# A mixture of experts whose first eight pairs' rows are scattered to two planes in memory and read back

## The chip, the core and the metric

The kernel runs on one core of one Trainium2 chip. The metric is the time on the device in microseconds (us), the median of several runs. A trace of one more execution is read with it.

## What is computed

A decoder block for 512 tokens of width 1024, float32. Two token mixers share one input projection, a sparse attention and a sliding-window attention; their gated sum goes through an output projection, a residual and a layer norm. Then comes the part that the change touches, a mixture of 32 experts in 4 groups. Each token takes its best group and in it its two best experts:

```python
g_sel = jnp.argmax(g_logits, axis=-1)
top_p, top_i = lax.top_k(e_prob, EXPERT_TOPK)            # 2 of the 8 experts of the group
top_w = g_w * top_p / top_p.sum(-1, keepdims=True)
expert_id = g_sel[:, None] * EXPERTS_PER_GROUP + top_i
...
for e in range(N_EXPERTS):
    h = jax.nn.silu(xt @ w_gate[e]) * (xt @ w_up[e])
    out = out + combine[:, e:e + 1] * (h @ w_down[e])
...
x = layer_norm(ALPHA * x + ffn, ln2_g[layer], ln2_b[layer])
```

## The kernel before

Attention and router take the first 415 us or so. They matter here only where the start of the program is spoken of: the input arrives as `xraw` and `wraw`, the index keys of the sparse attention are written to `pgA` and copied to the other 64 partitions by a transfer (`pgA<-pgA`), and the index scores (`qk<-pgA,qs`) read them.

**Experts.** Experts w and w+16 are a pair, and a pair is a job: each expert has 64 slots, so a job has 128 rows. The jobs run in the order 0 to 7, an overflow tile `ov` for tokens over 64, 8 to 15. The list `work` holds that order, n is the place in it: pair 9 is n = 10. For a job

- `gather` (GpSimd) reads the 128 slots' rows of `x1d` from memory by an index per slot; a slot without a token has an index past the end;
- `transposed` turns them on TensorE in eight transposes (`qt<-ident,xg`), and ScalarE copies them out as `xg`;
- `up_proj` makes 32 products (`mm<-wexp,xg`) with the two experts' gate and up weights, ScalarE takes SiLU, VectorE multiplies (`h`);
- `turn_hidden` turns `h` in two transposes (`mm<-ident,h`), ScalarE copies out `hT`;
- `down_half`, twice, makes 16 products (`pv<-wexp,hT`);
- the rows go back to their tokens by products too: `down_proj` splits the weighted rows into two parts `yh` and `yl`, `places` makes a matrix `ct` of zeros and ones (which slot holds which token), and `combine` multiplies, `qt<-yh,ct` and `qt<-yl,ct`, for four blocks of 128 tokens and two halves: 16 products and eight adds into the residual `acc` on VectorE. These eight parts, the list `late`, run inside the next job: HEAD = 4 after its up products, four after its hidden transposes.

**Weights.** Each expert's weights are three pages of 1 MiB, two up and one down, so a job has four up and two down loads. They are issued by SyncE in the order of use, three jobs ahead (`stage`), into a ring of 22 pages that also holds all else; a load waits until a page's last reader has passed. Banks tagged `qt` (four) hold the transposed rows and the combining products in turn.

**Order.** Inside an engine a scheduler fixes the order of instructions when the program is built; in time an engine runs them strictly in that order. DMAs of one queue start in the order of issue.

Of the kernel before, what the change touches and what calls it, by code (L numbers as in the profile page):

```python
# [10 lines left out]
F32 = mybir.dt.float32  # L11
# [9 lines left out]
P = 128  # L21
D = 1024
T = 512
# [45 lines left out]
KEEP1 = 15  # L69
KEEP1_E = ('tensor', 'scalar', 'vector')  # L70
HEAD = 4
LAST_N = (0, 1, 1, 2, 1, 2, 1, 0)
P_TR = 0
P_UP = 0
# [51 lines left out]
def block_kernel(ctx: ExitStack, tc: tile.TileContext, xT, x, w_tm, w_in, w_uv, w_br, w_out, relb, oh,  # L126
# [17 lines left out]
    def mm_bank():  # L144
        return bank("mm", 2)
# [104 lines left out]
    nc.vector.memset(ones, 1.0)  # L250
    rank4 = const.tile([P, 4], F32, name="rank4")
    nc.vector.tensor_scalar(rank4, iot[:, 0:4], -1.0, 5.0, op0=ALU.mult, op1=ALU.add)
    info = const.tile([P, NB, 16, 5], BF16, name="info")
    nc.vector.tensor_copy(info[:, :, :, 0:1], part1[:, None, None, :].to_broadcast([P, NB, 16, 1]))
    for b in range(NB):
        nc.vector.memset(info[:, b, :, 1:2], float(b))
    ident = const.tile([P, P], F32, name="ident")
# [16 lines left out]
    drb = dram.tile([8, 384], F32, name="drb")  # L274
    ska = dram.tile([8, P, 256], F32, name="ska")
    skb = dram.tile([8, P, 512], F32, name="skb")


    w_load_upto(1)
# [409 lines left out]
    for h in range(8):  # L689
        if h + 1 < 8:  # L690
            need(f"q{h + 1}")
            lg[h + 1] = dsa_logits(h + 1)
        if h and h % 2 == 0:
            dsa_up(h // 2 - 1)
        if h in BR_AT:
            br_load(BR_AT.index(h))
        for j in PREP_AT.get(h, ()):
            br_prep(j)
        dsa_out(h, lg.pop(h))
    fill(2)  # L700
    dsa_up(3)
# [39 lines left out]


    sel = const.tile([P, NB, NE], BF16, name="sel")
    wts = const.tile([P, NB, NE], F32, name="wts")
    key = const.tile([P, NB, NE], F32, name="key")
    lgt = const.tile([P, NB, 36], F32, name="lgt")
    lgm = const.tile([P, NB, NE], F32, name="lgm")
    tops = const.tile([P, 2, NB], F32, name="tops")
    wrt = const.tile([P, KC, 36], F32, name="wrt")
    nc.sync.dma_start(wrt, w_rt.rearrange("p (k c) -> p k c", k=KC))  # L750
# [148 lines left out]
    def route_weights():  # L899
# [18 lines left out]
        for c in range(3):  # L918
            nc.vector.tensor_copy(info[:, :, :, 2 + c], wp)
            if c < 2:  # L920
                nc.vector.tensor_sub(wp, wp, info[:, :, :, 2 + c])

    tok = const.tile([P, 16], F32, name="tok")
    wsl = const.tile([P, 16], F32, name="wsl")
    idx = const.tile([P, 16], I32, name="idx")

    def slots(i0, i1, weighted=True):

        pi = qk_bank()
        v = small.tile([P, 2, 8], F32, name="sl", bufs=2)  # L930
        c = slice(i0, i1)
        Gs = []

        def collect(a, n):
            for i, G in enumerate(Gs):
                for b in range(NB):
                    nc.tensor.matmul(pi[:, i * 8 + a:i * 8 + n], G[:, b], info[:, b, i0 + i, a:n], start=(b == 0),
                                     stop=(b == NB - 1))
            nc.vector.tensor_copy(v[:, :, a:n], pi[:, 0:16].rearrange("p (i c) -> p i c", c=8)[:, :, a:n])

        def weights():
            nc.vector.tensor_add(wsl[:, c], v[:, :, 2], v[:, :, 3])
            nc.vector.tensor_add(wsl[:, c], wsl[:, c], v[:, :, 4])

        for i in range(i0, i1):
            G = temp(BF16, "G")[:, 0:T].rearrange("p (b s) -> p b s", b=NB)
            kv = key.rearrange("p b (s e) -> p b s e", s=2)[:, :, :, i:i + 1]
            nc.vector.tensor_tensor(G.rearrange("p b (s c) -> p b s c", s=2),
                                    iot[:, None, None, 0:CAP].to_broadcast([P, NB, 2, CAP]),
                                    kv.to_broadcast([P, NB, 2, CAP]), ALU.is_equal)  # L950
            Gs.append(G)
        collect(0, 5 if weighted else 2)
        nc.vector.scalar_tensor_tensor(tok[:, c], v[:, :, 1], 128.0, v[:, :, 0], op0=ALU.mult, op1=ALU.add)
        nc.vector.tensor_scalar(v[:, :, 5], tok[:, c], 0.0, 4096.0, op0=ALU.is_equal, op1=ALU.mult)
        nc.vector.scalar_tensor_tensor(idx[:, c], tok[:, c], -1.0, v[:, :, 5], op0=ALU.add, op1=ALU.add)
        if weighted:
            weights()
        else:
            return lambda: (collect(2, 5), weights())

    x1d = dram.tile([T, D], F32, name="x1d")
    first = [pv_bank(), pv_bank()]
# [19 lines left out]
    def run(parts, n):  # L982
        for _ in range(n):
            if parts:
                parts.pop(0)()
# [70 lines left out]

    def gather(ix, m=P):

        pg = xgs[len(gathers) % 3]
        nc.gpsimd.memset(pg, 0.0)  # L1060
        gathers.append(nc.gpsimd.indirect_dma_start(out=pg[0:m], out_offset=None, in_=x1d[:, :],
                                                    in_offset=bass.IndirectOffsetOnAxis(ap=ix, axis=0),
                                                    bounds_check=T - 1, oob_is_err=False))
        return pg
# [16 lines left out]
            banks.append(tp)  # L1081
        return evac_x(banks, xgs[3])

    def up_proj(xt, up, ph=None, parts=(), counts=LAST_N, w_=None):

        ph = ph or mm_bank()
        for k in range(KC):
            for s in range(2):
                c = (k % 4) * T
                if len(up) == 2:  # L1090
                    Pinned(P_UP).matmul(ph[s * 64:(s + 1) * 64], xt[k][:, s * 64:(s + 1) * 64], up[s][k // 4][:, c:c + T],
                                     start=(k == 0), stop=(k == KC - 1))
                else:
                    Pinned(P_UP).matmul(ph[s * 64:(s + 1) * 64, 0:256], xt[k][:, 0:64],
                                     up[0][k // 4][:, c + s * 256:c + (s + 1) * 256],
                                     start=(k == 0), stop=(k == KC - 1))
            run(parts, counts[k])
        h = temp(F32, "h")
        if len(up) == 2:
            nc.scalar.activation(h[:, 0:256], ph[:, 0:256], AF.Silu)  # L1100
            if w_ is None:
                nc.vector.tensor_mul(h[:, 0:256], h[:, 0:256], ph[:, 256:512])  # L1102
            else:
                nc.vector.scalar_tensor_tensor(h[:, 0:256], h[:, 0:256], w_, ph[:, 256:512], op0=ALU.mult, op1=ALU.mult)
            return h[:, 0:256]
        h = h[64:128, 0:256]
        nc.scalar.activation(h, ph[0:64, 0:256], AF.Silu)
        nc.vector.tensor_mul(h, h, ph[64:128, 0:256])
        return h

    def turn_hidden(h, n):
        m = n * CAP
# [19 lines left out]
    def down_proj(hT, dn, w_):  # L1132
# [21 lines left out]
            r.append((yy,))  # L1154
        return r

    def places(tk_):
        ct = temp(F32R, "ct", "pt")
        nc.vector.tensor_scalar(ct, iot, tk_, None, op0=ALU.is_equal)
        return ct  # L1160
# [30 lines left out]

    def overflow_tiles():

        pn = mm_bank()
        for b in range(NB):
            nc.tensor.matmul(pn[:, 0:NE], ones, sel[:, b], start=(b == 0), stop=(b == NB - 1))
        nc.vector.tensor_copy(cnt, pn[:, 0:NE])
# [21 lines left out]
    def overflow_tile(j):  # L1219
# [21 lines left out]
        for c, m_ in enumerate((og, ow)):  # L1241
            nc.vector.tensor_add(m_[:, :, 0], m_[:, :, 0], m_[:, :, 1])
            nc.vector.tensor_copy(m_[:, :, 1], m_[:, :, 0])
            po = mm_bank()
            for b in range(NB):
                nc.tensor.matmul(po[:, 0:2], m_[:, b].rearrange("p z c -> p (z c)"), tv[:, b], start=(b == 0), stop=(b == NB - 1))
            nc.vector.tensor_copy(so[:, c:c + 1], po[:, c:c + 1])
        nc.vector.tensor_scalar(so[0:CAP, 2:3], so[0:CAP, 0:1], 0.0, 4096.0, op0=ALU.is_equal, op1=ALU.mult)
        io = small.tile([P, 1], I32, name="ovi_", bufs=1)
        nc.vector.scalar_tensor_tensor(io[0:CAP], so[0:CAP, 0:1], -1.0, so[0:CAP, 2:3], op0=ALU.add, op1=ALU.add)  # L1250
        pg = gather(io[0:CAP, 0:1], CAP)
        up = [page(F32, "wup") for _ in range(2)]
        dn = page(F32, "wdn")
        for q in range(2):
# [13 lines left out]
    def stage(w):  # L1268
        if w == "ov":
            jobs[w] = overflow_tile(0.0)  # L1270
        else:
            pg = None
            if w:
                pg = gather(idx[:, w:w + 1])
            if w == 15:
                load_pieces(6 * w + G2_AT)
                nc.sync.dma_start(g2[:, 0:D], bcast(ln2_g, D))
# [2 lines left out]
            es = (w, w + 16)  # L1280
            jobs[w] = (pg, [ups[e] for e in es], [dns[e] for e in es], tok[:, w:w + 1], wsl[:, w:w + 1])

    for w in work[:2]:
        stage(w)
    route_weights()
    weights()
    slots(2, 4)
    stage(work[2])
    late = []
    sums = small.tile([P, NB, 2], F32, name="sums", bufs=1)  # L1290
    mv4 = small.tile([P, 4, NB + 1], F32, name="mv4", bufs=1)
# [52 lines left out]
    def rest(pz, fresh=False):  # L1344
# [25 lines left out]
        for hf in range(2):  # L1370
# [4 lines left out]
        nc.gpsimd.indirect_dma_start(out=out[:, :], out_offset=bass.IndirectOffsetOnAxis(ap=idx[:, 15:16], axis=0),  # L1375
                                     in_=zs[:, 0:D], in_offset=None, bounds_check=T - 1, oob_is_err=False)

    for n, w in enumerate(work):
        if n % 2 == 0 and 4 + n < 16:
            slots(4 + n, 6 + n)  # L1380
# [3 lines left out]
            g2 = page(F32, "ln2")  # L1384
        if n + 3 < len(work):
            stage(work[n + 3])
        pg, up, dn, tk_, w_ = jobs.pop(w)
        last = n + 1 == len(work)
        if last:

# [5 lines left out]
            zb = [page(F32, "zb") for _ in range(2)]  # L1396
            z4 = [zb[b // 2][:, (b % 2) * D:(b % 2 + 1) * D] for b in range(NB)]
            pz = [tr_bank() for _ in range(2)]
        h = up_proj(xt.pop(w), up, None if n else pv_bank(), late if last else (), LAST_N, w_ if last else None)
        run(late, KC if last else HEAD)  # L1400
        if last:
            if DEV_E == 1:
                deviations(slice(0, 2))
            pick(pz, [0])
        if n < TR_FIRST:
            xt[work[n + 1]] = transposed(jobs[work[n + 1]][0], 1)
        hT = turn_hidden(h, len(up))
        run(late, KC)
        if last and DEV_E == 2:
            deviations(slice(0, 2))  # L1410
        if not last:
            if work[n + 1] not in xt:
                xt[work[n + 1]] = transposed(jobs[work[n + 1]][0], n >= PIN_N or n in PIN_S)
            y = down_proj(hT, dn, w_)
            late = combine(places(tk_), y, then if n + 2 == len(work) else None)
    pick(pz, [1], [0])
    for hf in range(2):
        down_half(hT, dn, hf, pz[hf])
# [6 lines left out]
    nov = nc.values_load(novi[0:1, 0:1], min_val=0, max_val=15)  # L1425
    with tc.For_i(1, nov, 1):
        o = overflow_tile(jc)
        y = down_proj(turn_hidden(up_proj(transposed(o[0]), o[1]), 1), o[2], o[4])
        parts_of.clear()
        run(combine(places(o[3]), y, then), 8)  # L1430
        pz = [tr_bank() for _ in range(2)]
# [93 lines left out]
```

## Time and profile before

| | us |
|---|---|
| median of 3 runs (710.46 to 710.7) | 710.65 |
| the profiled execution | 711.01 |
| its span in the trace | 709.2 |
| TensorE busy | 679.0 (96%) |
| VectorE busy | 430.3 (61%) |
| ScalarE busy | 268.2 (38%) |
| GpSimd busy | 83.9 (12%) |

The busy shares are means over the whole span. In the experts, from about 420 us to 690 us, the 16 DMA engines are busy too, which this table does not show.

### The profile page before, as it was taken

To read this page: it belongs to the slowest core of one execution; us is meant where nothing else is said; L and a number is where in the kernel's file an instruction comes from. 1 tells how busy PE (TensorE), PEld (TensorE's weight loads), DVE (VectorE), ACT (ScalarE), POOL (GpSimd) and SP (SyncE) were. 2 spreads that over 40 slices of the span, in tenths; PEclk is the share of its full clock that TensorE was granted. 3 is DMA by queue.
4 is the path that set the end of the run, shared out by engine and by line. 5 is a ranking of instruction groups with operands and counts; after the bars stand their busy time and mean duration, and the time that the engine had idled before them with its cause. 6 is when DMAs were issued, how large, how long until landed. Compare 5 with 4: busy or idle time off the path is not lost.

```text
span 709.2 us, 9623 instructions
## 1 busy us (share of the span) xinstructions
PE 679.0 (96%) x3522; PEld 459.3 (65%) x3522; DVE 430.3 (61%) x1018; ACT 268.2 (38%) x560; POOL 83.9 (12%) x85
## 2 busy tenths in 40 slices
PE   8999998999999999999999989999999999999991
PEld 4898886766688878778899964444544535444430
DVE  5785999857444444567716982855555555544575
ACT  5663422857264545743314231222122222222170
POOL 0100000000000000012200442111111111110073
PEclk9999999999999999999999999999999999999996
DMA  8372511011511111144966679999999999996003
GB/s 315 138 252 75 192 61 59 2 60 59 178 60 60 61 60 59 60 157 151 377 267 278 242 263 358 414 422 419 406 384 402 367 384 406 419 420 274 0 1 138
DMA packets 28287, 154.24 MB, mean 217 GB/s; under 512 B 5132, under 2 KB 6420, under 8 KB 12365
## 3 DMA queue, kind: packets, MB, share of 16 engines
q1 hardware_dynamic: 21324, 139.59, 50.1%
q0 software_dynamic: 4816, 10.86, 4.3%
q10 hardware_dynamic: 2096, 3.15, 1.3%
q8 instruction: 29, 0.48, 0.3%
q14 instruction: 22, 0.17, 0.1%
HBM read 152.42 MB, written 7.90 MB: 226 GB/s over the span
## 4 chain that ended last, share of the span: by engine, by line
PE 82%; DVE 13%; issue 1%; ACT 1%; DMA 1%; POOL 1%; POOLq 0%; SPq 0%; DVEq 0%; ACTq 0%
PE mm L1053 15%; PE qt L1053 10%; PE mm L172 10%; PE mm L174 9%; PE mm L173 9%; PE pv L1053 9%; DVE pgS L415 3%; DVE mx L413 2%; PE pv L545 2%; PE tr L626 1%; DVE whl L169 1%; DVE zb L105 1%; PE qk L173 1%; PE tr L531 1%; PE qk L174 1%
## 5 line engine op out<-in xcount | busy, mean ns | idle before, releaser
L172 PE MATMUL mm<-xh,whl 128*128 128x512 f32 (+1 forms) x272 | 108.9, 400 | 1.1 <-ACT xh L168 1.1
L173 PE MATMUL mm<-xl,whl 128*128 128x512 f32 (+1 forms) x272 | 106.7, 392 | 0.8 <-DVE xl L169 0.8
L174 PE MATMUL mm<-xh,whl 128*128 128x512 f32 (+1 forms) x272 | 106.3, 391 | 0.0
L1053 PE MATMUL mm<-wexp,xg 128*64 128x512 f32 x448 | 99.8, 593 | 0.0
L1170 DVE TENSOR_TENSOR acc<-acc,qt 128x512 f32<-128x512 f32 x120 | 73.1, 680 | 4.4 <-PE qt L1053 4.3
L1053 PEld LDWEIGHTS mm<-wexp,xg 128*64 128x64 f32 x448 | 33.0, 137 | 60.2 <-issue 59.9
L172 PEld LDWEIGHTS mm<-xh,whl 128*128 128x128 f32 x272 | 51.9, 191 | 13.3 <-issue 3.5
L174 PEld LDWEIGHTS mm<-xh,whl 128*128 128x128 f32 x272 | 51.8, 190 | 11.4 <-issue 1.6
L173 PEld LDWEIGHTS mm<-xl,whl 128*128 128x128 f32 x272 | 51.9, 191 | 10.7 <-issue 1.7
L169 DVE TENSOR_TENSOR whl<-wraw,whl 128x1024 fp32r<-128x1024 f32 x34 | 41.5, 1220 | 24.7 <-ACT whl L168 22.9
L1053 PE MATMUL pv<-wexp,hT 128*64 128x512 f32 x240 | 54.9, 598 | 0.0
L782 POOL TENSOR_TENSOR tg<-tg 128x512 f32<-128x512 f32 x8 | 12.1, 1515 | 302.9 <-DVE tg L684 302.9
L1102 DVE TENSOR_TENSOR h<-h,mm 128x256 f32<-128x256 f32 x14 | 5.9, 421 | 68.4 <-ACT h L1100 68.4
L1053 PE MATMUL qt<-yh,ct 128*128 128x512 f32 x112 | 46.8, 418 | 0.0
L1053 PE MATMUL qt<-yl,ct 128*128 128x512 f32 x112 | 44.1, 394 | 0.0
L1140 DVE SCALAR_TENSOR_TENSOR yl<-pv,wsl,yh 128x512 fp32r<-128x512 f32 x30 | 22.5, 750 | 34.4 <-ACT yh L1139 34.4
L168 ACT ACTIVATE whl<-wraw 128x1024 fp32r<-128x1024 f32 x34 | 35.7, 1054 | 13.7 <-DMA wraw<-in_w_in_dram 7.3
L1100 ACT ACTIVATE h<-mm 128x256 f32<-128x256 f32 x14 | 5.4, 384 | 88.8 <-PE mm L1053 88.8
L172 PE MATMUL mm<-woh,merged 128*128 128x256 f32 x120 | 36.3, 302 | 0.0
L1053 PEld LDWEIGHTS pv<-wexp,hT 128*64 128x64 f32 x240 | 16.5, 136 | 28.1 <-issue 27.6
L174 PE MATMUL mm<-woh,merged 128*128 128x256 f32 x120 | 34.0, 283 | 0.0
L173 PE MATMUL mm<-wol,merged 128*128 128x256 f32 x120 | 34.0, 283 | 0.0
(375 smaller groups left out, 1322.2 us busy)
## 6 DMA issues: line engine op xcount, KB each, us to landing
wexp<-in_w_up_dram SPq DMA_DIRECT2D x64, 1024.0 KB, 10.3
wexp<-in_w_dn_dram SPq DMA_DIRECT2D x31, 1024.0 KB, 9.4
wraw<-in_w_in_dram SPq DMA_DIRECT2D x16, 1024.0 KB, 4.9
braw<-in_w_br_dram SPq DMA_DIRECT2D x4, 1024.0 KB, 4.8
woraw<-in_w_out_dram SPq DMA_DIRECT2D x4, 1024.0 KB, 4.9
xraw<-in_xT_dram SPq DMA_DIRECT2D x4, 512.0 KB, 7.4
skb<-dra POOLq DMA_DIRECT2D x1, 2048.0 KB, 18.1
bias<-skb ACTq DMA_DIRECT2D x2, 1024.0 KB, 5.5
```

The lines of the kernel that those rows point to most:

```text
L168: nc.scalar.activation(hi, raw, AF.Copy)
L169: nc.vector.tensor_sub(lo, raw, hi.bitcast(F32))
L172: nc.tensor.matmul(o, a[0], b[0], start=start, stop=False)
L173: nc.tensor.matmul(o, a[0], b[1], start=False, stop=False)
L174: nc.tensor.matmul(o, a[1], b[0], start=False, stop=stop)
L413: pin(nc.vector.max(out=mx, in_=acc))
L415: pin(nc.vector.match_replace(out=acc, in_to_replace=mx, in_values=acc, imm_value=GONE))
L545: nc.tensor.matmul(py[g * 64:(g + 1) * 64], vb[:, b + 1 - n // P + s, g * 64:(g + 1) * 64], pts[s, g], start=(s == 0), stop=(s == n // P - 1))
L782: nc.gpsimd.tensor_add(u[0], u[0], u[1])
L1053: return lambda *a, **k: (pin if self.n else (lambda i: i))(getattr(nc.tensor, f)(*a, **k))
L1140: nc.vector.scalar_tensor_tensor(yl_, py, w_, yh_.bitcast(F32), op0=ALU.mult, op1=ALU.subtract)
L1170: nc.vector.tensor_add(a, a, pc)
```

## The change

The rows of pairs 0 to 7 (SCATTER) go back to their tokens through memory. A tensor `yp` of 1024 rows has two planes of 512 tokens. VectorE computes for every slot whether its expert is the token's first or second (a running sum over the pairs, `info[..., 5]`), and from that the row `place`. `scattered` weights a job's 128 rows into `y` and GpSimd writes them to `yp` by index; slots without a token have an index past the end. The planes are filled with zeros first, by eight transfers whose source is the still empty `routes`. After n = 10 and n = 11 (BACK_AT) `back_load` reads half of both planes into two pages each, and `back_add`, one job later, adds them to `acc` on VectorE. Pairs 8 to 15 and the overflow tile combine by products as before.

Where a job has no `late` parts, the next job's rows are turned between its up products and its hidden transposes, and the first k step of the next job's up products (K_EARLY = 1, four products) comes between the hidden transposes and the down products. Gathers use two buffers in turn instead of three, the third is `y`; a gather is issued behind the transposes that free its buffer (`fetch`).

```diff
+SCATTER = tuple(range(8))
+K_EARLY = 1
+BACK_AT = 10
...
+    yp = dram.tile([2 * T, D], F32, name="yp")
...
+        nc.sync.dma_start(yp[h * P:(h + 1) * P].rearrange("p (c d) -> p c d", c=4),
+                          zero[:, None, :].to_broadcast([P, 4, 256]))
         dsa_out(h, lg.pop(h))
...
+        nc.vector.tensor_tensor(wp, sel[:, :, 0:16], sel[:, :, 16:32], ALU.add)
+        cum = small.tile([P, NB, 16], F32, name="cum", bufs=1)
+        flat = [t.rearrange("p b i -> p (b i)") for t in (cum, same, wp)]
+        nc.vector.tensor_tensor_scan(flat[0], flat[1], flat[2], 0.0, op0=ALU.mult, op1=ALU.add)
+        nc.vector.tensor_sub(info[:, :, :, 5], cum, wp)
...
-        pg = xgs[len(gathers) % 3]
+        pg = xgs[len(gathers) % 2]
...
+    def scattered(w, hT, dn, w_):
+
+        y = xgs[2]
+        for hf in range(2):
+            py = down_half(hT, dn, hf)
+            c = y[:, hf * T:(hf + 1) * T]
+            if hf == 0:
+                nc.scalar.activation(c, py, AF.Copy, scale=w_)
+            else:
+                nc.vector.tensor_scalar(c, py, w_, None, op0=ALU.mult)
+        nc.gpsimd.indirect_dma_start(out=yp[:, :], out_offset=bass.IndirectOffsetOnAxis(ap=place[:, w:w + 1], axis=0),
+                                     in_=y, in_offset=None, bounds_check=2 * T - 1, oob_is_err=False)
+
+    def back_load(q):
+        r = []
+        for z in range(2):
+            t = page(F32, "back")
+            a = z * T + q * 2 * P
+            nc.sync.dma_start(t.rearrange("p (b d) -> p b d", b=2), yp[a:a + 2 * P].rearrange("(b p) d -> p b d", p=P))
+            r.append(t)
+        return r
+
+    def back_add(q, r):
+        for b in range(2):
+            for t in r:
+                a = acc[2 * q + b]
+                nc.vector.tensor_add(a, a, t[:, b * D:(b + 1) * D])
...
-        if n < TR_FIRST:
-            xt[work[n + 1]] = transposed(jobs[work[n + 1]][0], 1)
+        nx = None if last else work[n + 1]
+        ahead = not last and not late
+        if ahead:
+            xt[nx] = transposed(rows_of.pop(nx), 1)
+            if n + 3 < len(work):
+                fetch(work[n + 3])
         hT = turn_hidden(h, len(up))
         run(late, KC)
...
+        if ahead:
+            early[n + 1] = mm_bank()
+            up_part(early[n + 1], xt[nx], jobs[nx][1], range(K_EARLY))
+            done_early = True
...
+            if w in SCATTER:
+                scattered(w, hT, dn, w_)
+                late = []
+            else:
+                y = down_proj(hT, dn, w_)
+                late = combine(places(tk_), y, then if n + 2 == len(work) else None)
+        for q in range(2):
+            if n == BACK_AT + q:
+                back[q] = back_load(q)
+            if n == BACK_AT + q + 1:
+                back_add(q, back.pop(q))
```

How the order of instructions moves, at three places. The first is VectorE, before, from the hidden product `h` of one late pair to that of the next; the adds `acc<-acc,qt` belong to the job before:

```order
L1102 TENSOR_TENSOR h<-h,mm 128x256
L1170 TENSOR_TENSOR acc<-acc,qt 128x512 x8
L1140 SCALAR_TENSOR_TENSOR yl<-pv,wsl,yh 128x512 x2
L1159 TENSOR_SCALAR ct<-iot,tok 128x512
L1102 TENSOR_TENSOR h<-h,mm 128x256
```

And after the change, from pair 11's hidden product into pair 12's job; `acc<-acc,back` are the new adds:

```order
L1126 TENSOR_TENSOR h<-h,mm 128x256
L1212 TENSOR_TENSOR acc<-acc,back 128x1024 x4
L1227 TENSOR_TENSOR acc<-acc,qt 128x512 x8
L1169 SCALAR_TENSOR_TENSOR yl<-pv,wsl,yh 128x512 x2
L1216 TENSOR_SCALAR ct<-iot,tok 128x512
L1126 TENSOR_TENSOR h<-h,mm 128x256
L1227 TENSOR_TENSOR acc<-acc,qt 128x512 x4
L1212 TENSOR_TENSOR acc<-acc,back 128x1024 x4
L1227 TENSOR_TENSOR acc<-acc,qt 128x512 x4
```

Four adds of `back` now stand ahead of the eight in pair 11's job, and four between the fourth and the fifth in pair 12's.

The second is SyncE's queue after the change, from pair 12's up loads on (`in_w_up_dram` and `in_w_dn_dram` are the up and down weights):

```order
L751 DMA wexp<-in_w_up_dram 128x2048 x4
L754 DMA wexp<-in_w_dn_dram 128x2048 x2
L1204 DMA back<-yp 128x2x1024 x2
L751 DMA wexp<-in_w_up_dram 128x2048 x4
L754 DMA wexp<-in_w_dn_dram 128x2048 x2
L1204 DMA back<-yp 128x2x1024 x2
L751 DMA wexp<-in_w_up_dram 128x2048 x4
```

Before, the same queue has only the loads, four up and two down in turn; now two loads of `back` stand behind pair 12's weights and two behind pair 13's.

The third is the start of SyncE's queue; `pgA<-pgA` is the copy of the index keys. Before:

```order
L305 DMA relx<-in_relb_dram 32x16
L750 DMA wrt<-in_w_rt_dram 128x288
L752 DMA ln1c<-in_ln_t_dram 128x16
L304 DMA tmraw<-in_w_tm_dram 128x2048
L306 DMA ohp<-in_oh_dram 33x1024
L327 DMA pgA<-pgA 64x1024
```

And after the change, where `yp<-routes` are the zero fills:

```order
L319 DMA relx<-in_relb_dram 32x16
L713 DMA yp<-routes 512x1x256
L318 DMA tmraw<-in_w_tm_dram 128x2048
L320 DMA ohp<-in_oh_dram 33x1024
L713 DMA yp<-routes 512x1x256 x2
L341 DMA pgA<-pgA 64x1024
L192 DMA wraw<-in_w_in_dram 128x2048
L713 DMA yp<-routes 512x1x256 x5
L764 DMA wrt<-in_w_rt_dram 128x288
```

Three fills stand ahead of the copy and five behind the load after it; the load of `wrt` moved behind them.

In the code the fills stand in the loop over the heads of the sparse attention; nothing holds them back there, and the scheduler moved them up.

## Rows read from the trace of the kernel before

**Rows 1.** Chain of waits: start us, length us, engine, operation, line.

```profile
436.84 6.78 PE mm L1053 x30
...
608.36 6.87 PE mm L1053 x32
...
624.02 6.87 PE mm L1053 x32
```

**Rows 2.** Timeline of TensorE (PE) in pair 12: start us, length us, instruction, count.

```profile
630.82 0.50 PE L1053 MATMUL qt<-yh,ct 128*128 128x512 f32 x1
...
632.77 0.38 PE L1053 MATMUL mm<-ident,h 128*128 128x128 f32 x2
632.91 0.48 PE L1053 MATMUL qt<-yh,ct 128*128 128x512 f32 x1
...
634.84 1.25 PE L1053 MATMUL qt<-ident,xg 128*128 128x128 f32 x8
636.02 3.65 PE L1053 MATMUL pv<-wexp,hT 128*64 128x512 f32 x16
```

**Rows 3.** Waits of SyncE's queue: us in total, times, longest us.

```profile
SPq L735 <- PE mm L1053: 53.9, 23, 3.1
SPq L738 <- PE pv L1053: 52.0, 7, 8.0
```

**Rows 4.** Busy time by stretch; the last three columns: TensorE's clock, DMA share, GB/s.

```profile
470.00:490.00 20.00, 20.00 (x102) 8.73 (x100) 9.32 (x22) 3.34 (x6) 2.22 (x2) 1.00 1.02 419
610.00:630.00 20.00, 20.00 (x98) 8.74 (x96) 7.40 (x13) 3.34 (x6) 1.95 (x2) 1.00 1.01 418
```

**Rows 5.** Timeline of VectorE (DVE) in pair 12.

```profile
631.38 0.42 DVE L1102 TENSOR_TENSOR h<-h,mm 128x256 f32<-128x256 f32 x1 [5.42 <-ACT h L1100]
631.71 4.86 DVE L1170 TENSOR_TENSOR acc<-acc,qt 128x512 f32<-128x512 f32 x8
```

**Rows 6.** Queues, 460 to 470, then twice 480 to 490 us: packets, MB, share.

```profile
q1 hardware_dynamic: 579, 4.22, 101.0%
...
q1 hardware_dynamic: 523, 3.80, 91.7%
q0 software_dynamic: 144, 0.36, 9.3%
```

**Rows 7.** Down loads of pairs 3 and 12: issue, and time to landing.

```profile
436.87 0.80 SPq L738 DMA_DIRECT2D wexp<-in_w_dn_dram  x2
DMA to landing us min/median/max: 9.9/10.1/10.3
...
592.72 0.80 SPq L738 DMA_DIRECT2D wexp<-in_w_dn_dram  x2
DMA to landing us min/median/max: 7.6/8.6/9.6
```

**Rows 8.** The page's groups: an add of 128x1024 on VectorE, xcount | busy, mean ns.

```profile
L169 DVE TENSOR_TENSOR whl<-wraw,whl 128x1024 fp32r<-128x1024 f32 x34 | 41.5, 1220 | 24.7 <-ACT whl L168 22.9
```

**Rows 9.** Busy time by stretch where the router ends (first TensorE; third from last its clock).

```profile
414.00:415.00 1.00, 0.00 (x0) 0.00 (x0) 0.97 (x3) 0.00 (x0) 0.71 (x1) 1.00 1.02 426
416.00:417.00 1.00, 1.00 (x9) 0.95 (x8) 1.00 (x4) 0.67 (x2) 0.57 (x1) 0.82 0.02 8
417.00:420.00 3.00, 3.00 (x16) 2.98 (x15) 1.56 (x5) 1.73 (x3) 2.39 (x4) 0.50 0.69 227
420.00:421.00 1.00, 1.00 (x14) 0.60 (x13) 0.74 (x3) 0.60 (x1) 0.00 (x0) 0.97 0.99 385
```

**Rows 10.** The start: stretches, the queue in 12 to 18 us, the key copy, its reader.

```profile
17.00:18.00 1.00, 1.00 (x8) 1.00 (x7) 0.89 (x2) 1.00 (x2) 0.00 (x0) 1.00 0.34 119
18.00:19.00 1.00, 1.00 (x7) 1.00 (x7) 0.73 (x2) 0.97 (x2) 0.00 (x0) 1.00 0.00 0
...
q1 hardware_dynamic: 905, 2.05, 91.1%
...
18.29 0.55 SPq L327 DMA_DIRECT2D pgA<-pgA  x1
DMA to landing us min/median/max: 3.1/3.1/3.1
...
22.90 0.28 PE L385 MATMUL qk<-pgA,qs 128*128 128x256 f32 x1
```

More of the change, by code (lines that the diff above doesn't have):

```diff
@@ L252, in block_kernel @@
     nc.vector.tensor_scalar(rank4, iot[:, 0:4], -1.0, 5.0, op0=ALU.mult, op1=ALU.add)
-    info = const.tile([P, NB, 16, 5], BF16, name="info")
+    info = const.tile([P, NB, 16, 6], BF16, name="info")
     nc.vector.tensor_copy(info[:, :, :, 0:1], part1[:, None, None, :].to_broadcast([P, NB, 16, 1]))
+    routes = const.tile([P, 3, NB, NE], F32, name="routes")
+    nc.vector.memset(routes, 0.0)
+    zero = routes[:, 0:2].rearrange("p z b e -> p (z b e)")
+    same = const.tile([P, NB, 16], F32, name="same")
+    nc.vector.memset(same, 1.0)
+    nc.vector.memset(same[:, :, 0:1], 0.0)
     for b in range(NB):
@@ L743, in block_kernel @@
     sel = const.tile([P, NB, NE], BF16, name="sel")
-    wts = const.tile([P, NB, NE], F32, name="wts")
-    key = const.tile([P, NB, NE], F32, name="key")
+    wts, key, lgm = (routes[:, z] for z in range(3))
     lgt = const.tile([P, NB, 36], F32, name="lgt")
-    lgm = const.tile([P, NB, NE], F32, name="lgm")
     tops = const.tile([P, 2, NB], F32, name="tops")
@@ L925, in block_kernel @@
     idx = const.tile([P, 16], I32, name="idx")
+    place = const.tile([P, 16], I32, name="place")
     def slots(i0, i1, weighted=True):
@@ L943, in weights @@
             nc.vector.tensor_add(wsl[:, c], wsl[:, c], v[:, :, 4])
+            nc.vector.scalar_tensor_tensor(v[:, :, 6], v[:, :, 5], float(T), v[:, :, 6], op0=ALU.mult, op1=ALU.add)
+            nc.vector.scalar_tensor_tensor(place[:, c], tok[:, c], -1.0, v[:, :, 6], op0=ALU.add, op1=ALU.add)
         for i in range(i0, i1):
@@ L951, in slots @@
             Gs.append(G)
-        collect(0, 5 if weighted else 2)
+        collect(0, 6 if weighted else 2)
         nc.vector.scalar_tensor_tensor(tok[:, c], v[:, :, 1], 128.0, v[:, :, 0], op0=ALU.mult, op1=ALU.add)
-        nc.vector.tensor_scalar(v[:, :, 5], tok[:, c], 0.0, 4096.0, op0=ALU.is_equal, op1=ALU.mult)
-        nc.vector.scalar_tensor_tensor(idx[:, c], tok[:, c], -1.0, v[:, :, 5], op0=ALU.add, op1=ALU.add)
+        nc.vector.tensor_scalar(v[:, :, 6], tok[:, c], 0.0, 4096.0, op0=ALU.is_equal, op1=ALU.mult)
+        nc.vector.scalar_tensor_tensor(idx[:, c], tok[:, c], -1.0, v[:, :, 6], op0=ALU.add, op1=ALU.add)
         if weighted:
@@ L958, in slots @@
         else:
-            return lambda: (collect(2, 5), weights())
+            return lambda: (collect(2, 6), weights())
     x1d = dram.tile([T, D], F32, name="x1d")
@@ L1082, in transposed, with up_part @@
         return evac_x(banks, xgs[3])
-    def up_proj(xt, up, ph=None, parts=(), counts=LAST_N, w_=None):
-        ph = ph or mm_bank()
-        for k in range(KC):
+    def up_part(ph, xt, up, ks, parts=(), counts=LAST_N):
+        for k in ks:
             for s in range(2):
@@ L1097, in up_proj, with hidden @@
             run(parts, counts[k])
+    def hidden(ph, up, w_=None):
         h = temp(F32, "h")
@@ L1109, in up_proj @@
         return h
+    def up_proj(xt, up):
+        ph = mm_bank()
+        up_part(ph, xt, up, range(KC))
+        return hidden(ph, up)
     def turn_hidden(h, n):
@@ L1192, in overflow_tiles @@
     def overflow_tiles():
-        pn = mm_bank()
+        pn = qk_bank()
         for b in range(NB):
@@ L1243, in overflow_tile @@
             nc.vector.tensor_copy(m_[:, :, 1], m_[:, :, 0])
-            po = mm_bank()
+            po = qk_bank()
             for b in range(NB):
@@ L1250, in overflow_tile @@
         nc.vector.scalar_tensor_tensor(io[0:CAP], so[0:CAP, 0:1], -1.0, so[0:CAP, 2:3], op0=ALU.add, op1=ALU.add)
-        pg = gather(io[0:CAP, 0:1], CAP)
+        pg = functools.partial(gather, io[0:CAP, 0:1], CAP)
         up = [page(F32, "wup") for _ in range(2)]
@@ L1271, in stage @@
         else:
-            pg = None
-            if w:
-                pg = gather(idx[:, w:w + 1])
+            pg = functools.partial(gather, idx[:, w:w + 1]) if w else None
             if w == 15:
@@ L1281, in stage, with fetch @@
             jobs[w] = (pg, [ups[e] for e in es], [dns[e] for e in es], tok[:, w:w + 1], wsl[:, w:w + 1])
+    rows_of = {}
+    def fetch(w):
+        rows_of[w] = jobs[w][0]()
     for w in work[:2]:
         stage(w)
+    fetch(work[1])
     route_weights()
@@ L1288, in block_kernel @@
     stage(work[2])
+    fetch(work[2])
     late = []
@@ L1376, in rest @@
                                      in_=zs[:, 0:D], in_offset=None, bounds_check=T - 1, oob_is_err=False)
+    early, back, done_early = {}, {}, False
     for n, w in enumerate(work):
@@ L1386, in block_kernel @@
             stage(work[n + 3])
-        pg, up, dn, tk_, w_ = jobs.pop(w)
+        _, up, dn, tk_, w_ = jobs.pop(w)
         last = n + 1 == len(work)
@@ L1398, in block_kernel @@
             pz = [tr_bank() for _ in range(2)]
-        h = up_proj(xt.pop(w), up, None if n else pv_bank(), late if last else (), LAST_N, w_ if last else None)
+        ph = early.pop(n) if n in early else mm_bank() if n else pv_bank()
+        up_part(ph, xt[w], up, range(K_EARLY if n and done_early else 0, KC), late if last else (), LAST_N)
+        done_early = False
+        xt.pop(w)
+        h = hidden(ph, up, w_ if last else None)
         run(late, KC if last else HEAD)
@@ L1410, in block_kernel @@
             deviations(slice(0, 2))
+        if ahead:
+            early[n + 1] = mm_bank()
+            up_part(early[n + 1], xt[nx], jobs[nx][1], range(K_EARLY))
+            done_early = True
         if not last:
[L1412 to L1415, printed above, removed]
+            if nx not in xt:
+                xt[nx] = transposed(rows_of.pop(nx), n >= PIN_N or n in PIN_S)
+                if n + 3 < len(work):
+                    fetch(work[n + 3])
+            if w in SCATTER:
[9 more added lines that the diff above has]
+                back_add(q, back.pop(q))
     pick(pz, [1], [0])
@@ L1427, in block_kernel @@
         o = overflow_tile(jc)
-        y = down_proj(turn_hidden(up_proj(transposed(o[0]), o[1]), 1), o[2], o[4])
+        y = down_proj(turn_hidden(up_proj(transposed(o[0]()), o[1]), 1), o[2], o[4])
         parts_of.clear()
```

## The prediction

> **What bounds the kernel now.** I read the chain of waits first. From 436.84 us on it is TensorE work without a gap: one pair of experts every 15.66 us, pair 11 starting at 608.36 and pair 12 at 624.02 [rows 1]. Inside such a pair the timeline of TensorE shows what the change takes out: eight products from 630.82 to 632.77 and eight from 632.91 to 634.84, 1.95 + 1.93 = 3.9 us of 15.66 [rows 2]. So TensorE is the bound, and SyncE's queue agrees: its weight loads wait for TensorE to give pages back [rows 3].
>
> Then I read the memory side, because the change adds traffic there. The 16 DMA engines are busy for 1.02 and 1.01 of the stretches 470 to 490 and 610 to 630 us, at 419 and 418 GB/s [rows 4]. A pair's six loads of 1.0486 MB and its gathered rows are 6.29 + 0.26 = 6.55 MB, which is 418 GB/s over 15.66 us. The kernel therefore has two bounds within a per cent of each other: a pair cannot go faster than its weights arrive, whatever TensorE is relieved of. What TensorE has is a lead: pair 3's down weights are issued as pair 1 begins [rows 1, 7].
>
> **What is removed.** Pairs 0 to 7 lose their 16 products each: 8 x 3.9 = 31.2 us of TensorE, and VectorE loses 8 x 8 adds. The products also covered the wait for SiLU and for the turned hidden rows. The eight transposes of the next rows (1.2 us, 634.84 to 636.02 [rows 2]) and the first four products of the next pair take that place. In before the hidden rows are turned 1.95 us after the first combining product began, but VectorE's product that they need ends at 631.80, 1.0 us after it [rows 2, 5]; the transposes cover that, and I cost this at nothing (if the cover failed, up to 0.5 us a pair, which the wait below would hide).
> Were this all, pair 11 would start at 608.36 - 31.2 = 577.2.
>
> **What is added on the memory side.** (a) Eight scatters. Only valid rows move: the gather in 480 to 490 us, pair 7's, is 0.36 MB [rows 6], and the reference's routing gives that pair 89 rows of 4 KB, 0.36 MB, not 128. The same routing gives 498 rows for pairs 0 to 7, so 2.04 MB are written. (b) Four loads `back` of 1.05 MB, two after pair 12's weights and two after pair 13's in SyncE's queue. (c) Eight zero fills at the start.
>
> **Where it hurts.** VectorE's order puts the first four adds of `back` behind the hidden product of pair 11 and ahead of the eight adds that free the banks of pair 11's combining products. So TensorE halts in pair 11 until `back` has landed. In before VectorE's first such add starts 631.71 - 624.02 = 7.7 us into a pair [rows 1, 5]; TensorE's own pace would want `back` at 577.2 + 7.7 = 584.9. When can it be there? Everything ahead of it in the queue must have moved:
> - pair 3's last down load is issued at 437.3 and takes 10.1 us: 447.4 [rows 7];
> - behind it stand 57 weight loads (pairs 4 to 12 at six, the overflow's three). At 418 GB/s one takes 2.51 us: 143.1. TensorE gives pages back earlier than before, so I assume no gap;
> - ten gathers, 581 rows, 2.38 MB. The row-wise queue moved 0.36 MB in 9.3% of 10 us, 0.39 MB per us [rows 6]: 6.1;
> - the scatters' 2.04 MB, for which before has no row: at the gathers' rate 5.2;
> - the two `back` loads, in 4 KB lines as the gathers are: 2.10 MB, 5.4.
> Sum: 447.4 + 143.1 + 6.1 + 5.2 + 5.4 = **607.2 us**, 22 us after TensorE could use it. The 31 us are not gained; they become this wait. As the wait is set by bytes, the details of the first eight pairs cost nothing.
>
> Bounds: loads at 422 GB/s (4.22 MB in 460 to 470 [rows 6]) give 605.7. Before's own pace, gaps included, is (593.2 + 9.6 - 447.4 - 6.1) / 57 = 2.62 us a load [rows 7] and gives 613.4. I stay near the first, since the gaps of before came from pages not yet free.
>
> The Trainium skill (DMA: Bandwidth & Descriptors, Specifications) gives one core about 358 GB/s of HBM; by that a load would take 2.93 us, `back` would land near 631 and the kernel would take about 737. The rows at 418 disagree, and the sum goes by them.
>
> **After the wait.** Half of the adds can run as the first `back` lands; two remain, at 1.22 us for 128x1024 [rows 8]: VectorE goes on at 609.6. In before it was there at 608.36 + 7.7 = 616.1, so pair 11 is 6.4 us early. TensorE has then stood still for over 20 us. In before, after it stood still in 414 to 415 us, its granted clock was 0.82 in 416 to 417, 0.50 (1.2 GHz) in 417 to 420 and 0.97 in 420 to 421 [rows 9]: 0.18 + 3 x 0.50 + 0.03 = 1.7 us of its work lost. So 4.7 early. The second `back` lands six loads, two `back` and a gather later: 15.1 + 5.4 + 0.6 = 21.1, at 628.3. In pair 12 VectorE reaches it after four of its adds (4.86 us for eight [rows 5]) at 624.02 + 7.7 + 2.4 - 4.7 = 629.4, so it has landed, but its four adds, 4.9 us, stand ahead of the adds that free banks for the transposes: 0.2 late. That halt may cost the clock again, 1.7: 1.9 late. For this I have only that one place; without either drop it is 3.4 less. Pairs 13 to 15 and the end are as before.
>
> **The start.** Three zero fills now stand ahead of the copy of the index keys. The queue was empty at about 17.3 us and the copy, issued at 18.29, took 3.1 [rows 10]. 1.57 MB more, less 0.15 for a load that moves back, at 2.05 MB per 5.5 us [rows 10] make 3.8 us: empty at 21.1, copy landed by 24.2. The first product that reads it ran at 22.90; four products of 0.17 us are put ahead of it, so the halt is about 0.6. With the three added vector operations ahead of the first pair's slots I take 1.0 in all; if small lines cost double, 4.5. The other five fills drain under stretches in which the queue was idle.
>
> **Sum.** 711.0 us (the profiled execution) + 1.9 + 1.0 = 713.9; the median of the runs shown is 0.36 lower, so **713.5 us**, 0.4% slower.
>
> **Rivals.**
> 1. *Faster: the transfers have room.* If `back` landed by 584.9, nearly all of the 31.2 us would stay, less 9.8 for VectorE's eight adds: about 690. For it: SyncE waits for pages, never for transfers [rows 3]. Against it: 57 loads would have to run at 490 GB/s. What is possible is a part: at 422 GB/s, no clock lost, no halt at the start: 713.5 - 1.5 - 3.4 - 1.0 = 707.6. It decides in favour of a gain if `back` lands before about 603.
> 2. *No change:* as the sum, with one clock drop or none: 709 to 712.
> 3. *Much slower: mixed traffic moves at before's own pace.* `back` lands at 613.4, the second 0.7 later still: 713.5 + 6.9 = 720. For it: 57 loads took that long in before. Against it: then the queue had gaps.
> 4. *The start:* the fills delay the index keys by 4.5 instead of 1.0: 717.
>
> **How the numbers follow.** Forecast, with rival 4 as its upper part, 45%; rival 3, 17%; rival 2, 18%; rival 1, 20% (16 of them for the part, 4 for all of it). A difference under 0.2%, 1.4 us, is what a measurement of this kernel cannot tell from none. Faster 0.20, same 0.18, slower 0.62. The range goes from the partial gain to before's pace: 707 to 721; the likeliest case alone is 712 to 717.
>
> **What would show it.** Right: pairs 1 to 7 about 12 us apart in the chain; TensorE idle for some 20 us in pair 11, released by VectorE's adds of `back`, which wait for the DMA; DMA share near 1.0 from 450 to 660; `back` landing near 607. Wrong: `back` landed before VectorE asks for it, DMA engines idle between 450 and 600, or TensorE still 15.7 us a pair in the first eight, with another wait named.

## The result, and the profile after

| | before | after |
|---|---|---|
| median of 6 runs, us | 710.49 (708.59 to 710.70) | 715.95 (713.77 to 718.41) |
| the profiled execution, us | 711.01 | 714.15 |
| its span, us | 709.2 | 712.3 |
| TensorE busy, us | 679.0 | 650.9 |

The changed kernel is slower: ratio 1.0077, 95% interval 1.0055 to 1.0099. TensorE lost 28 us of work, and the end did not come earlier.

The chain of waits of the changed kernel: start us, length us, what.

```profile
435.84 6.01 PE mm L1076 x28
...
450.85 16.74 DMA wexp<-in_w_up_dram
...
579.68 6.87 PE mm L1076 x32
...
588.51 19.98 DMA back<-yp
608.59 1.28 DVE acc L1212 x2
611.60 4.36 PE qt L1076 x16
...
619.55 6.92 PE mm L1076 x32
629.63 3.54 DVE acc L1212 x4
...
641.21 6.87 PE mm L1076 x32
```

Up to pair 11 (579.68) the saving is there: 608.36 before [rows 1]. Then the chain leaves TensorE for the read back, which lands at 588.51 + 19.98 = 608.5, and comes back to pair 12 at 619.55, 40 us after pair 11 began. A second, short stop is the four adds at 629.63. Pair 13 starts at 641.21; before, it was 624.02 + 15.66 = 639.68.

VectorE in pairs 11 and 12 (timeline; in brackets idle us and what ended it):

```profile
587.03 0.42 DVE L1126 TENSOR_TENSOR h<-h,mm 128x256 f32<-128x256 f32 x1 [5.42 <-ACT h L1124]
606.06 2.36 DVE L1212 TENSOR_TENSOR acc<-acc,back 128x1024 f32<-128x1024 f32 x2 [18.61 <-DMA back<-yp]
608.59 2.36 DVE L1212 TENSOR_TENSOR acc<-acc,back 128x1024 f32<-128x1024 f32 x2 [0.17 <-DMA back<-yp]
610.87 4.99 DVE L1227 TENSOR_TENSOR acc<-acc,qt 128x512 f32<-128x512 f32 x8
...
627.24 2.47 DVE L1227 TENSOR_TENSOR acc<-acc,qt 128x512 f32<-128x512 f32 x4
629.63 4.62 DVE L1212 TENSOR_TENSOR acc<-acc,back 128x1024 f32<-128x1024 f32 x4
```

VectorE is through with `h` at 587.45 and stands 18.61 us for the first page of `back` and again for the second. The eight adds that free the banks start at 610.87. In pair 12 the pages are there already (no bracket); what costs there is the adds' own 4.62 us in front of four others. TensorE's largest row of waits (us in total, times, longest us) is these two places:

```profile
PE qt L1076 <- DVE acc L1227: 27.2, 2, 22.8
```

And its timeline where it starts again, in pair 11 and in pair 12:

```profile
611.60 0.80 PE L1076 MATMUL qt<-yh,ct 128*128 128x512 f32 x1 [22.79 <-DVE acc L1227]
...
614.93 1.04 PE L1076 MATMUL qt<-ident,xg 128*128 128x128 f32 x8
...
634.90 1.83 PE L1076 MATMUL qt<-ident,xg 128*128 128x128 f32 x8 [4.38 <-DVE acc L1227]
636.66 4.55 PE L1076 MATMUL pv<-wexp,hT 128*64 128x512 f32 x16
```

Products and transposes just behind a stop are longer than elsewhere (0.80 and 0.63 us against 0.40 for a combining product): the granted clock is at its lower level, 0.50, from 595 to 614 us and again from 636 to 638.

Busy time by stretch (engines in the order PE, PEld, DVE, ACT, POOL; then TensorE's clock, DMA share, GB/s):

```profile
450.00:470.00 20.00, 20.00 (x100) 7.53 (x98) 6.80 (x26) 4.18 (x9) 5.27 (x6) 1.00 1.02 419
...
600.00:610.00 10.00, 0.00 (x0) 0.00 (x0) 3.77 (x4) 0.00 (x0) 0.00 (x0) 0.50 1.02 417
610.00:620.00 10.00, 8.40 (x36) 4.91 (x38) 6.57 (x10) 2.15 (x4) 1.95 (x2) 0.77 1.01 419
...
630.00:640.00 10.00, 5.62 (x23) 2.64 (x23) 6.64 (x8) 1.65 (x3) 1.95 (x2) 0.83 1.01 419
```

The DMA engines are full in all of them, also while TensorE does nothing, and its clock falls to 0.50, 1.2 GHz. SyncE's queue says the same: from 440 to 660 us its loads wait above all for earlier loads to land (below), where before they waited for TensorE to give pages back [rows 3].

```profile
SPq L751 <- DMA wexp<-in_w_up_dram: 52.5, 24, 2.9
```

Before, the DMA engines were as full in single stretches [rows 4] but not in all: from 450 to 600 us they moved 59.77 MB before and 62.72 after.

### The profile page after: what moved, and what is told of

Read it like the earlier page. It is cut to its first block, busy times and chain, and to the rows that moved or that the text cites. A ratio compares the mean times of both kernels' runs of the same rounds, so it can differ in the third digit from the quotient of the medians.

```text
span 712.3 us, 9305 instructions
## 1 busy us (share of the span) xinstructions
PE 650.9 (91%) x3394; PEld 435.8 (61%) x3394; DVE 394.5 (55%) x968; ACT 261.3 (37%) x552; POOL 90.9 (13%) x93
## 3 DMA queue, kind: packets, MB, share of 16 engines
q0 software_dynamic: 5968, 12.90, 5.1%
## 4 chain that ended last, share of the span: by engine, by line
PE 65%; DMA 16%; DVE 14%; issue 2%; ACT 1%; POOL 1%; POOLq 0%; SPq 0%; DVEq 0%; ACTq 0%
PE mm L177 10%; PE mm L179 9%; PE mm L178 9%; DMA wexp<-in_w_up_dram 9%; PE mm L1076 8%; PE pv L1076 5%; PE qt L1076 4%; DMA wexp<-in_w_dn_dram 3%; DMA back<-yp 3%; DVE pgS L429 3%; DVE mx L427 2%; PE pv L559 2%; DVE whl L174 1%; PE tr L640 1%; DVE zb L110 1%
## 5 line engine op out<-in xcount | busy, mean ns | idle before, releaser
L1076 PE MATMUL mm<-wexp,xg 128*64 128x512 f32 x448 | 102.7, 595 | 1.8 <-DMA wexp<-in_w_up_dram 1.8
L1076 PE MATMUL qt<-yh,ct 128*128 128x512 f32 x48 | 21.0, 437 | 22.8 <-DVE acc L1227 22.8
L1227 DVE TENSOR_TENSOR acc<-acc,qt 128x512 f32<-128x512 f32 x56 | 34.3, 679 | 5.2 <-PE qt L1076 5.2
L1093 ACT ACTIVATE xg<-qt 128x512 f32<-128x512 f32 x32 | 18.0, 596 | 45.8 <-PE qt L1076 45.8
L1083 POOL MEMSET xg<- 128x1024 f32 x16 | 15.2, 953 | 137.0 <-PE qt L1076 137.0
```

Source lines behind the costliest of these rows:

```text
L1076: return lambda *a, **k: (pin if self.n else (lambda i: i))(getattr(nc.tensor, f)(*a, **k))
L1093: nc.scalar.activation(c, banks[q], AF.Copy)
L1227: nc.vector.tensor_add(a, a, pc)
```

## The experiments

The expectations count jobs by the place n in `work`: the changed kernel's adds are issued at the end of places 11 and 12, which are pairs 10 and 11, and run inside the job that follows.

**1. The same transfers, the adds two jobs later.**

```diff
+ADD_AT = 13
-            if n == BACK_AT + q + 1:
+            if n == ADD_AT + q:
                 back_add(q, back.pop(q))
```

> The two groups of four adds of what is read back stand at the end of pairs 13 and 14 instead of 11 and 12; bytes, loads and their order stay. If the wait is a matter of where VectorE wants the rows (the prediction's step: they land some 22 us after VectorE could use them, and everything behind the adds stands still), it goes away: the pages land near 608 as before, VectorE reaches the adds at about 626 and waits for nothing, and the end is then set by the landing of pair 15's weights at about 650 (pair 15 started near 672 in the changed kernel): 687 to 695 us. Rival, that the transfers' bytes set the end whatever VectorE does (the DMA queues stay full to 657 and something else waits in the adds' place): 708 to 716 us.

Measured 696.04 us, ratio 0.9797 (0.9779 to 0.9815). The same bytes in the same order are 20 us faster, so the bytes alone do not make the changed kernel slow; the rival falls. Timeline of VectorE in pair 12 and of TensorE in pairs 13 and 15:

```profile
604.73 4.86 DVE L1228 TENSOR_TENSOR acc<-acc,qt 128x512 f32<-128x512 f32 x8
609.51 1.22 DVE L1213 TENSOR_TENSOR acc<-acc,back 128x1024 f32<-128x1024 f32 x1
...
615.70 4.74 PE L1077 MATMUL mm<-wexp,xg 128*64 128x512 f32 x16 [1.51 <-DMA wexp<-in_w_up_dram]
...
654.10 1.89 PE L111 MATMUL mm<-wexp,xg 128*64 128x512 f32 x8
```

No add waits. The expectation had VectorE at the adds near 626; the scheduler set the first group earlier, at 609.5, but behind pair 12's eight adds. The new bound is the one named: weights. Pair 15 starts at 654.10 where 650 was expected, and the time is 1 us above the range.

**2. Reads and adds both two jobs earlier.** `BACK_AT = 8` instead of 10.

> The read back and its adds are moved two pairs earlier together (reads behind pairs 8 and 9, adds at the end of 9 and 10). By the prediction's step the wait only moves: the reads land two pairs' weights, 12 x 2.51 = 30 us, earlier, and are wanted 2 x 15.7 = 31 us earlier, so VectorE waits about 20 us in pair 9 instead of 11, and the time is 713 to 719 us. Rival, that the reads were simply too late in the queue and that an earlier place gives them a landing in time: the wait goes and the time is 690 to 700 us.

716.49 us, 1.0071 (1.0048 to 1.0094), as the changed kernel.

```profile
575.17 2.36 DVE L1212 TENSOR_TENSOR acc<-acc,back 128x1024 f32<-128x1024 f32 x2 [18.07 <-DMA back<-yp]
```

The wait moved to pair 9 and kept its length (18.61 there). So the rival, that a read placed earlier would be in time, falls: what counts is the distance from the read's place in the queue to the add, not the place.

**3. Four pairs scattered.** `SCATTER = tuple(range(4))`.

> Only the first four pairs are scattered, pairs 4 to 7 are combined by TensorE as in the kernel before; the read back is whole. TensorE gets 4 x 3.9 = 15.6 us of products back, four scatters of 0.5 MB less go through the queues (about 1.25 us each, 5 us). By the prediction's step TensorE's saved time was only turned into the wait, so half of it given back costs nothing: pair 11's adds are reached at about 603, the reads land at 603 to 605, and the time is 708 to 712 us, under the changed kernel's. Rival, that the removed products count for the end: half of the work back makes it slower by up to 15 us, 720 to 730 us.

711.56 us, 1.0020 (1.0005 to 1.0036).

```profile
604.07 2.36 DVE L1212 TENSOR_TENSOR acc<-acc,back 128x1024 f32<-128x1024 f32 x2 [4.82 <-DMA back<-yp]
606.59 2.36 DVE L1212 TENSOR_TENSOR acc<-acc,back 128x1024 f32<-128x1024 f32 x2 [0.15 <-DMA back<-yp]
```

The rival falls: TensorE got half of its products back and the kernel became faster, by 4.4 us in the medians (715.95 to 711.56) and 2.3 in the spans (712.3 to 710.0). VectorE's wait went from 18.61 to 4.82 us. The second page landed 2 us earlier (606.5, not 608.5); four scatters are 0.98 MB less in the row-wise queue (11.92 against 12.90 MB), 2.5 us at the rate of the prediction. The expectation's 0.5 MB a scatter was twice too much, here and in experiments 6 and 7.

**4. No read back, no adds.** The four lines after `for q in range(2)` are removed.

> The rows are scattered but never read back nor added, so the first eight pairs' part is missing from the output; both the 4.2 MB of reads (about 10 us of the queues) and VectorE's wait go. By the prediction's step the end is set by the landing of pair 15's weights, 10 us earlier than in the changed kernel (about 642): 680 to 687 us. Rival, that the eight scatters and the lost clock are what costs: 700 us or more stays without the read back.

684.30 us, 0.9634 (0.9602 to 0.9666). The scatters stay, so the rival, that they and the clock cost, falls. The start of pair 15 in TensorE's timeline:

```profile
644.46 1.89 PE L110 MATMUL mm<-wexp,xg 128*64 128x512 f32 x8
```

And busy time from 480 to 640 us:

```profile
480.00:640.00 160.00, 155.34 (x766) 72.22 (x765) 61.55 (x129) 31.76 (x60) 22.93 (x23) 1.00 1.01 418
```

Pair 15 starts 9.6 us before that of experiment 1; the four reads, 4.19 MB at 418 GB/s, are 10.0. With the wait gone, these bytes are paid at the end.

**5. The adds one job later.** As experiment 1, with `ADD_AT = 12`.

> The adds at the end of pairs 12 and 13, one pair later than in the changed kernel and one earlier than in the first experiment. By the theory that the wait is the landing less the time at which VectorE is ready, its 18.6 us shrink by one pair's 15.7 us: VectorE is ready at about 603 and waits 3 to 6 us, TensorE halts once for about as long, and since the weights' landing then sets the end as in the first experiment (696.0), little of it is left: 695 to 701 us. Rival, that any place before the last pairs stops TensorE for a whole round of transfers: above 705 us.

700.59 us, 0.9855 (0.9838 to 0.9871).

VectorE's timeline, and TensorE's waits:

```profile
608.98 2.36 DVE L1213 TENSOR_TENSOR acc<-acc,back 128x1024 f32<-128x1024 f32 x2 [3.25 <-DMA back<-yp]
```

```profile
PE qt L1077 <- DVE acc L1228: 11.8, 2, 7.4
```

VectorE waits 3.25 us, as expected, but TensorE waits 11.8 in two places, where one short halt was expected: here the groups of four stand ahead of pair 12's eight adds and amid pair 13's, as in the changed kernel. In experiment 1 they run in the same two pairs, but behind the eight, and TensorE waits for no add. So the place inside the pair was worth about 4.5 us (700.6 against 696.0).

**6, 7 and 9. The adds late, six, four and five pairs scattered.** Experiment 1 with `range(6)`, `range(4)` and `range(5)`.

> As the first experiment, but only six pairs are scattered: two pairs' products return (2 x 3.9 = 7.8 us of TensorE) and two scatters of 0.5 MB go (2.5 us of the queues). In the first experiment TensorE waited 6.3 us for weights between 600 and 660. If weights' landing and TensorE's work now limit about equally, the one gives back what the other takes: 692 to 697 us. Rival, that the end of the first experiment hangs on transfers alone: 693.5 us or less.

> As the first experiment, with four pairs scattered: 15.6 us of products return to TensorE, 5 us of scatters go. If, with the wait gone, TensorE's products count again, the time goes up against the first experiment (696.0): by 15.6 less the 6 to 8 us that TensorE waited there, 702 to 706 us. Rival, that the transfers set the end: 690 to 692 us.

> The adds late as in the first experiment, with five pairs scattered. TensorE alone would give the time of four (693.8) less one pair's products, 3.9: 689.9; the weights' landing that of six (691.7) or a little under. If these are the only two limits: 689 to 692 us, about as six. Rival, that a third limit stands behind them: 693 us or more.

| scattered, adds late | us | ratio to before |
|---|---|---|
| 8 (experiment 1) | 696.04 | 0.9797 (0.9779 to 0.9815) |
| 6 | 691.71 | 0.9740 (0.9724 to 0.9756) |
| 5 | 691.17 | 0.9733 (0.9702 to 0.9764) |
| 4 | 693.76 | 0.9763 (0.9746 to 0.9779) |

Five is as expected. Six came 0.3 us under its range and inside its rival's: the transfers alone still set the end, and TensorE waits for pair 14's weights (first fence). With four it waits for none, one pair every 15.66 us again (second fence), and its runs (693.50 to 694.11) all lie above those of six (690.68 to 692.74): there TensorE sets the end. So two limits cross between six and four; five and six can't be told apart.

```profile
PE mm L1077 <- DMA wexp<-in_w_up_dram: 3.4, 3, 1.3
```

```profile
606.72 7.04 PE L1077 MATMUL mm<-wexp,xg 128*64 128x512 f32 x32
622.38 7.04 PE L1077 MATMUL mm<-wexp,xg 128*64 128x512 f32 x32
638.04 7.04 PE L1077 MATMUL mm<-wexp,xg 128*64 128x512 f32 x32
653.69 1.89 PE L111 MATMUL mm<-wexp,xg 128*64 128x512 f32 x8
```

Four missed its expectation of 702 to 706. It rested on 6.3 us of idle time of TensorE between 600 and 660 in experiment 1. By start times TensorE had lost more: pair 15 starts at 654.10 there and at 653.69 here, though here 15.6 us more products have run. Part of that lay before the window: pair 9 starts at 549.50 there and at 559.70 here, 10.2 us apart where four pairs' products are 15.6. From pair 9 to pair 15 TensorE lost another 10.6 us, of which idle time shows 6.3. It hid part, since products that wait for weights show as long ones: sixteen at 615.70 took 4.74 us, where 32 take 7.04.

The fall from eight to six is larger than the bytes explain: 4.3 us in the medians, and pair 15 starts 3.7 us earlier (650.45; 0.55 of it because pair 1 did). The two scatters are 0.52 MB (12.90 against 12.38 MB in the row-wise queue), 1.3 us at the rate of the prediction. Why the rest came is open, as in experiment 8.

**8. Every scatter twice**, the second into a tensor `yp2` that nothing reads:

```diff
+        nc.gpsimd.indirect_dma_start(out=yp2[:, :], out_offset=bass.IndirectOffsetOnAxis(ap=place[:, w:w + 1], axis=0),
+                                     in_=y, in_offset=None, bounds_check=2 * T - 1, oob_is_err=False)
```

> The changed kernel, with every scatter issued a second time into a second tensor that nothing reads: 2.04 MB more of row-wise writes ahead of the read back, and nothing else on TensorE or VectorE. It measures the price that the prediction had no row for. At the gathers' rate, as the prediction took it, the read back lands 5.2 us later than in the changed kernel (608.5 us), at about 614, and the time is 5 us up, 718 to 722 us. If written rows cost the queues twice that (leaving out four scatters moved the landing by about 5 us, where 0.98 MB at the gathers' rate would be 2.5), it lands near 619 and the time is 723 to 728 us. Rival, that the writes run beside the loads for nothing: 714 to 717 us.

724.81 us, 1.0226 (1.0186 to 1.0265), 8.9 us above the changed kernel.

VectorE's timeline where the second page lands:

```profile
617.67 2.36 DVE L1215 TENSOR_TENSOR acc<-acc,back 128x1024 f32<-128x1024 f32 x2 [0.17 <-DMA back<-yp]
```

That is 617.6, 9.1 later than in the changed kernel, and the time follows it, into the second range of the expectation (723 to 728). The row-wise queue from 420 us to this landing (packets, MB, share of the 16 engines), and ScalarE's (ACT) largest wait from 430 to 560 us:

```profile
q0 software_dynamic: 4391, 8.49, 11.4%
```

```profile
ACT xg L1194 <- DMA yp<-xg,place: 46.5, 6, 10.3
```

The same queue row of the changed kernel, from 420 to its landing at 608.5:

```profile
q0 software_dynamic: 3221, 6.30, 8.9%
```

11.4% of 197.6 us less 8.9% of 188.5 is 5.7 us of queue time for 2.19 MB, near the 5.2 that the prediction took; so that range's reason, that written rows cost the queues twice as much, is not what the queue shows. The 5 us that the expectation gives for leaving out four scatters was 2.0 in experiment 3. The other 3 us are weights: their queue had moved 1.28 MB more by the landing (71.73 against 70.45), 3.1 us at 418 GB/s. Why more of them went ahead of the read back is open. ScalarE now also waits for the single buffer `y`, 46.5 us in all, so this edit is not the price alone.

## Why the prediction was right

Forecast 713.9 profiled and 713.5 median, measured 714.15 and 715.95. Its central step, that `back` lands after VectorE wants it and the saved time becomes that wait, is shown by experiments 1 and 2: move the adds alone and the wait goes, move reads and adds together and it stays. Rival 1 (room in the transfers) fell: `back` landed at 608.5, not by 603, and the DMA share was full throughout. So did rival 3: its landing was 613.4. Rival 2, 709 to 712, needed one clock loss less; both were there. Of the rate: the Trainium skill (HBM Reference, Specifications (TRN2)) says that a core that streams alone measures about 425 GB/s, well above its share of 358 when both cores of a pair stream; the rows at 417 to 419 agree with the first.

Step by step:

- *Pair 11 at 577.2*: 579.51 in TensorE's timeline. The chain runs through weight loads from 450.85 on, and TensorE's first waits for weights stand in pair 8, from 528 us on (1.8 us of idle time there), so its lead was used up before pair 11, which the sum did not have; the wait hid it. VectorE was ready at 587.45, not 584.9.
- *`back` at 607.2, 22 us late*: 608.5, and from VectorE's readiness to the second page 21.1. The terms are right too: from 447.4 to 608.5 the row-wise queue moved 4.41 MB (4.42 in the sum, scatters included) and the other 62.83 MB (59 loads, 61.87), all at 418 GB/s. The details of the first eight pairs cost nothing, as said: experiment 3 gave half of them back and lost nothing.
- *VectorE goes on at 609.6*: 610.87.
- *The clock, 1.7 us twice*: the eight products after the stop took 614.93 - 611.60 = 3.33 us, where 1.93 is usual [rows 2], so 1.4; in the second stop eight transposes and sixteen down products took 1.83 + 4.55 in place of 1.25 + 3.65, so 1.5. The clock fell both times, as taken.
- *Pair 12 4.7 early, pair 13 1.9 late*: 624.02 - 619.55 = 4.5 early and 641.21 - 639.68 = 1.5 late.
- *The start, 1.0*: not seen. The copy of the keys, issued at 18.20, took 5.4 us and landed at 23.6 (24.2 forecast):

```profile
18.20 0.52 SPq L341 DMA_DIRECT2D pgA<-pgA  x1
...
23.30 0.34 PE L179 MATMUL mm<-xh,whl 128*128 128x384 f32 x1
23.76 0.35 PE L399 MATMUL qk<-pgA,qs 128*128 128x256 f32 x1
```

  A product every 0.18 us ends in a gap of 0.46, so the halt is 0.28 us, not 0.6; and pair 1 starts at 435.84 with 28 of its products to go, before at 436.84 with 30 [rows 1]. A single execution cannot show 1 us, though: with the same fills, pair 1's long row of products starts between 435.21 (experiment 6) and 437.32 (experiment 9), on both sides of 436.59 before. Rival 4, 4.5 us, is outside that spread and falls.
- *"The end as before"*: it was 1.6 us longer, 71.1 from pair 13's start against 69.5. The last output transfer on the chain, after and before:

```profile
699.90 3.54 DMA out_dram<-zb
```

```profile
698.37 2.62 DMA out_dram<-zb
```

  That is 0.9; 0.7 lies behind the last instruction on the chain. In the experiments this transfer took 2.62 to 4.43 us, so I put it down to spread; nothing was run on it. It took the place of the 1.0 of the start: two errors of about 0.2% cancel, and that the profiled time was met within 0.3 us is luck.
- *The median 0.36 under the profiled run*: it was 1.8 above it, with runs from 713.77 to 718.41; the profiled run was the second fastest of six. This is most of what the forecast was short. By and large the slower runs had the lower mean granted clock (0.971 in the fastest, 0.961 in the slowest), so the two stops may differ from run to run; only one of these runs has a trace, so that is not shown.

## What to carry to other kernels

When a kernel is within a per cent of both TensorE and its transfers, work moved from one to the other pays only until the limits cross: here, with the adds late, scattering five or six of the first eight pairs was the best of the four counts tried, 2.6 to 2.7% under before. Ask of each transfer where it stands in its queue and add up what is ahead of it; then put its reader behind that time, and behind the work in its engine's order on which others wait. The same transfers were 0.8% slower or 2% faster than no change by the place of eight adds.

## What the runs showed that I had not expected

- With a full queue a load took long to land here: `back` about 20 us from issue to landing, weights before 7.6 to 10.3 [rows 7].
- An engine's idle time understates a shortage of weights (experiments 1 and 7): compare start times.
- The adds' place inside a pair was worth 4.5 us, and it was set by the scheduler, not by the line in the code (experiments 1 and 5).
- A second set of scatters cost 8.9 us, 3 us more than its queue time: more weights had moved before the read back landed; why is open.
